# Row scales kept on chip, k's low parts doubled to 128 rows, and the q/k norm steps moved between engines

## The chip, the core and the metric

The kernel runs on one core of a Trainium2 chip. A core has TensorE (PE, matmuls; its weight loads are shown apart as PEld), VectorE (DVE), ScalarE (ACT), GpSimd (POOL) and SyncE (SP), which here only issues transfers. Engines run their own instructions in order and wait for each other by semaphores. The metric is device time in microseconds for one execution; lower is better. Beside it stands a profile of one execution, with the start and length of each instruction.

## What is computed

One block on a sequence of 1024 tokens with 1024 features, in float32: a norm, a mixer made of stick-breaking attention and a gated linear recurrence, a second norm, and an MLP with a squared ReLU. Cut to what matters here:

```python
h = rms_norm(x, norm1_g)
q, k, v, xl, gl = split(h @ w_in)              # 512 features each
q = rms_norm(q per head of 64, q_norm_g)
k = rms_norm(k per head of 64, k_norm_g)
# per head, causal:
z = (q @ k.T) / sqrt(64)
w = sigmoid(z) * suffix_product(sigmoid(-z))   # where key < query
attn = w @ v
lru = rg_lru(conv(xl)) * gelu(gl)
x = x + concat(attn, lru) @ w_out
x = x + square(relu(rms_norm(x) @ w_up)) @ w_down
```

There are eight heads of 64 features. `rms_norm` multiplies by one over the root of the mean square.

## The kernel before

**Precision.** Most products are made from a high and a low part of each operand: a value is rounded to the matmul's format (the high part, a copy on ScalarE) and the remainder is the low part (`lo_part`, L60, a subtraction on VectorE or GpSimd). `mm3` (L70 to L73) then adds three matmuls: low by high, high by low, high by high.

**Stages.** First x is loaded, transposed and scaled (`norm1_pair`), and the q, k, v of the first pair of heads are made. Then comes the recurrent unit (`lru_tile`), whose result goes to DRAM (`lru_d`). Then comes a stage in which attention, the projections of the other three pairs and the gates are woven together: `ORDER` (L34) lists these pieces by hand, with `A` for one head and 256 queries, `I` for a projection of 256 tokens, `G` for a gate, `W` and `O` for weight loads and `Y` for sums of MLP weights made by transfers. Last come the output projection and the MLP. The framework places the instructions of each engine in an order of its own, worked out from its estimate of their times, so instructions of several pieces alternate on an engine.

**A projection step** (`in_proj`, four per pair of heads, 16 in all) works on 256 tokens:

- TensorE makes q, k, v for two tiles of 128 tokens (`pd`, L201); ScalarE copies q and k to `raw` with the row's scale (L203), and v's parts are taken at L205 and L206.
- VectorE squares `raw` (L209), sums over 64 features (L211) and runs `rsqrt_mean` (L88): a scale and a guess made from the bits (L92, L93), then three Newton steps of three operations each on eight columns (L95, L96, L97). VectorE then scales `raw` (L213), and GpSimd multiplies q by the gains (L214).
- q's high and low parts go side by side into 128 columns (`qs`). k's high part is written twice (`ks`, L222), its low part once (`kl`, L223, on GpSimd).
- TensorE transposes them (L228, L233, L237), and `qT`, `kH` and `kL` are copied out (L229, L234, L238). In `kL` the two heads lie one above the other, 64 rows each.

**Attention** (L414) makes `z` for 128 queries and up to 512 keys from two matmuls: L431 with all 128 rows (q's high and low parts by k's high part twice) and L432 with the head's 64 rows (q's high part by k's low part). On the diagonal L434 adds the mask. ScalarE takes two sigmoids (L436, L437), VectorE a running product (L441), GpSimd multiplies (L442), TensorE transposes the weights (L452), and L461 multiplies them with v.

**A gate** (L479) loads the 512 row scales of its tokens, spread over 128 partitions, from `rs_d` in DRAM (L483) into a buffer of the tag `raw`, loads the recurrent result (L484), projects (L485), scales (L487), and goes on with the gelu. The same row scales were held on chip as `rsb` (L353) during the recurrent unit and given up after it.

Of the kernel before, what the change touches and what calls it, by code (L numbers as in the profile page):

```python
# [9 lines left out]
F32 = mybir.dt.float32  # L10
F32R = mybir.dt.float32r
# [8 lines left out]
P = 128  # L20
# [23 lines left out]
def kernel(ctx, tc, x, norm1_g, w_in, conv_w, conv_b, w_rg, b_rg, w_ig, b_ig,  # L44
# [39 lines left out]
    def bank(pl, shape, name):  # L84
        return pl.tile([P] + shape, F32, tag=pl.name, name=name)


    def rsqrt_mean(ssq, n, cols):  # L88
        v = small.tile([P, 8], F32, tag="rs_v", name="rs_v")[:, :cols]
        y = small.tile([P, 8], F32, tag="rs_y", name="rs_y")[:, :cols]  # L90
        m = small.tile([P, 8], F32, tag="rs_m", name="rs_m")[:, :cols]
        nc.vector.tensor_scalar(v, ssq, 1.0 / n, EPS, op0=ALU.mult, op1=ALU.add)  # L92
        nc.vector.tensor_scalar(y.bitcast(I32), v.bitcast(I32), -0.5, float(0x5F3759DF), op0=ALU.mult, op1=ALU.add)  # L93
        for _ in range(3):
            nc.vector.scalar_tensor_tensor(m, y, -0.5, v, op0=ALU.mult, op1=ALU.mult)  # L95
            nc.vector.tensor_tensor(m, m, y, op=ALU.mult)  # L96
            nc.vector.scalar_tensor_tensor(y, m, 1.5, y, op0=ALU.add, op1=ALU.mult)  # L97
        return y
# [52 lines left out]
    hTh = hp.tile([P, KC, S], F32R, name="hTh")  # L151
    hTl = hp.tile([P, KC, S], F32R, name="hTl")
    qkvE = pool(left1, "qkvE")
    wp = pool(left1, "wp", bufs=8)
    mp = pool(left1, "misc")

# [31 lines left out]

    def in_proj_open(p, qp):
        return (qp.tile([P, 2, S], F32R, tag="qT", name=f"qT{p}"), qp.tile([P, 2, S], F32R, tag="kH", name=f"kH{p}"),  # L190
                qp.tile([P, S], F32R, tag="kL", name=f"kL{p}"), qp.tile([P, NT, 2, P], F32R, tag="vv", name=f"vv{p}"))

    def in_proj(p, qkv, ws, tp):
        qT, kH, kL, vv = qkv
        raw = mp.tile([P, 2, 4, HD], F32, tag="raw", name=f"raw{p}{tp}", bufs=2)
        for tt in range(2):
            t = 2 * tp + tt
            pd = bank(ps_d, [384], f"pd{p}{t}")
            for kc in range(KC):
                wh, wl = ws[kc]  # L200
                mm3(pd, hTh[:, kc, t * P:(t + 1) * P], hTl[:, kc, t * P:(t + 1) * P], wh, wl, kc == 0, kc == KC - 1)  # L201
            rs = rstd1[:, t:t + 1]
            nc.scalar.mul(raw[:, tt].rearrange("p a d -> p (a d)"), pd[:, 0:256], rs)  # L203
            pvv = pd[:, 256:384].rearrange("p (h d) -> p h d", h=2)
            nc.scalar.mul(vv[:, t, :, 0:HD], pvv, rs)  # L205
            nc.vector.scalar_tensor_tensor(vv[:, t, :, HD:P], pvv, rs, vv[:, t, :, 0:HD].bitcast(F32), op0=ALU.mult, op1=ALU.subtract)  # L206
        sq = mp.tile([P, 8, HD], F32, tag="sq", name=f"sq{p}{tp}")
        raw8 = raw.rearrange("p t a d -> p (t a) d")
        nc.vector.tensor_tensor(sq, raw8, raw8, op=ALU.mult)  # L209
        ssq = small.tile([P, 8], F32, tag="ssq8", name=f"ssq{p}{tp}")  # L210
        nc.vector.tensor_reduce(ssq, sq, axis=AX.X, op=ALU.add)  # L211
        rstd = rsqrt_mean(ssq, HD, 8)
        nc.vector.tensor_tensor(raw8, raw8, rstd.unsqueeze(2).broadcast_to([P, 8, HD]), op=ALU.mult)  # L213
        nc.gpsimd.tensor_tensor(raw[:, :, 0:2, :], raw[:, :, 0:2, :], qkg, op=ALU.mult)  # L214
        qs = mp.tile([P, 2, 2, 2, HD], F32R, tag="qs", name=f"qs{p}{tp}")
        ks = mp.tile([P, 4, 2, HD], F32R, tag="ks", name=f"ks{p}{tp}")
        kl = mp.tile([P, 2, 2, HD], F32R, tag="kl", name=f"kl{p}{tp}")
        for h in range(2):
            nc.scalar.copy(qs[:, :, h, h, :], raw[:, :, h, :])
            lo_part(nc.vector, qs[:, :, h, 1 - h, :], raw[:, :, h, :], qs[:, :, h, h, :])  # L220
        for tt in range(2):
            nc.scalar.copy(ks[:, 2 * tt:2 * tt + 2], raw[:, tt, 2:4, :].unsqueeze(2).broadcast_to([P, 2, 2, HD]))  # L222
            lo_part(nc.gpsimd, kl[:, tt], raw[:, tt, 2:4, :], ks[:, 2 * tt:2 * tt + 2, 0, :])  # L223
        cols = slice(256 * tp, 256 * tp + 256)
        pq = bank(ps_t, [2, 256], f"pq{p}{tp}")
        for h in range(2):
            for tt in range(2):
                nc.tensor.matmul(pq[:, h, tt * P:(tt + 1) * P], qs[:, tt, h].rearrange("p a d -> p (a d)"), identr, start=True, stop=True)  # L228
        nc.scalar.copy(qT[:, :, cols], pq)  # L229
        pk = bank(ps_t, [2, 256], f"pk{p}{tp}")  # L230
        for h in range(2):
            for tt in range(2):
                nc.tensor.matmul(pk[:, h, tt * P:(tt + 1) * P], ks[:, 2 * tt + h].rearrange("p a d -> p (a d)"), identr, start=True, stop=True)  # L233
        nc.vector.tensor_copy(kH[:, :, cols], pk)  # L234
        pl = bank(ps_t, [256], f"pl{p}{tp}")
        for tt in range(2):
            nc.tensor.matmul(pl[:, tt * P:(tt + 1) * P], kl[:, tt].rearrange("p a d -> p (a d)"), identr, start=True, stop=True)  # L237
        nc.vector.tensor_copy(kL[:, cols], pl)  # L238


    right1 = ExitStack()
# [108 lines left out]

    lstack = ExitStack()
    lp = pool(lstack, "lru", bufs=2, side="right")
    rsb = lp.tile([P, S], F32, name="rsb", bufs=1)  # L353
    for ch in range(2):
        nc.sync.dma_start(rsb[:, 512 * ch:512 * ch + 512], rs_row[:, 512 * ch:512 * ch + 512].broadcast_to([P, 512]))
    bd = {}
# [57 lines left out]
    def attention(p, h, c, qkv):  # L414
# [4 lines left out]
        for r in (2 * c, 2 * c + 1):  # L419
            n = (r + 1) * P  # L420
            wps = {}
            nxt = None
            qr = slice(r * P, (r + 1) * P)
            for k0 in range((n - 1) // 512 * 512, -1, -512):
                kn = min(n - k0, 512)
                diag = k0 + kn == n
                g = ap.tile([P, 516], F32, tag="g", name=f"g{p}{h}{r}{k0}", bufs=NG)
                w = ap.tile([P, 512], F32, tag="w", name=f"w{p}{h}{r}{k0}", bufs=NW)
                wps[k0 // 512] = w
                z = bank(ps_z, [512], f"z{p}{h}{r}{k0}")[:, :kn]  # L430
                nc.tensor.matmul(z, qT[:, h, qr], kH[:, h, k0:k0 + kn], start=True, stop=False)  # L431
                nc.tensor.matmul(z, qT[hs, h, qr], kL[hs, k0:k0 + kn], start=False, stop=not diag)  # L432
                if diag:
                    nc.tensor.matmul(z[:, kn - P:kn], identb, maskb, start=False, stop=True)  # L434
                    nc.gpsimd.memset(g[:, kn:kn + 1], 1.0)
                nc.scalar.activation(g[:, :kn], z, AF.Sigmoid, scale=-1.0)  # L436
                nc.scalar.activation(w[:, :kn], z, AF.Sigmoid)  # L437
                if not diag:
                    nc.vector.tensor_copy(g[:, kn:kn + 1], nxt)
                gr = g[:, :kn][:, ::-1]  # L440
                nc.vector.tensor_tensor_scan(gr, gr, gr, g[:, kn:kn + 1], op0=ALU.mult, op1=ALU.bypass)  # L441
                mark(nc.gpsimd.tensor_tensor(w[:, :kn], w[:, :kn], g[:, 1:kn + 1], op=ALU.mult))  # L442
                nxt = g[:, 0:1]
            wrow.append(wps)
# [34 lines left out]
    def gate(c, ch):  # L479
        s0 = 512 * ch  # L480
        y = mp.tile([P, 512], F32, tag="raw", name=f"gx{c}{ch}", bufs=2)
        hs = mp.tile([P, 512], F32, tag=("ks", "kl")[c % 2], name=f"hl{c}{ch}")
        nc.sync.dma_start(y, rs_row[:, s0:s0 + 512].broadcast_to([P, 512]))  # L483
# [3 lines left out]
        nc.vector.tensor_tensor(y, pd, y, op=ALU.mult)  # L487
# [387 lines left out]
```

## Time and profile before

| | us |
|---|---|
| three runs | 1215.89, 1217.34, 1218.22 |
| median | 1217.34 |
| profiled execution | 1218.14 |
| its span | 1216.4 |

| engine | busy, share of the span | instructions |
|---|---|---|
| TensorE | 95% | 5410 |
| its weight loads | 78% | 5410 |
| VectorE | 74% | 1182 |
| ScalarE | 47% | 991 |
| GpSimd | 48% | 472 |

The shares are means over stages with different limits. TensorE's granted clock is 0.969 of full speed on the mean. Matmuls are pipelined and their ends are modelled, so the records of neighbours overlap; what one costs is read from its start to the next one's start. Where a row names what an engine waited for, that is the semaphore that came last in the profile; "issue" is idle time for which the profile shows no wait.

### The profile page before, as it was taken

To read this page: it belongs to the slowest core of one execution; us is meant where nothing else is said; L and a number is where in the kernel's file an instruction comes from. 1 tells how busy PE (TensorE), PEld (TensorE's weight loads), DVE (VectorE), ACT (ScalarE), POOL (GpSimd) and SP (SyncE) were. 2 spreads that over 40 slices of the span, in tenths; PEclk is the share of its full clock that TensorE was granted. 3 is DMA by queue.
4 is the path that set the end of the run, shared out by engine and by line. 5 is a ranking of instruction groups with operands and counts; after the bars stand their busy time and mean duration, and the time that the engine had idled before them with its cause. 6 is when DMAs were issued, how large, how long until landed. Compare 5 with 4: busy or idle time off the path is not lost.

```text
span 1216.4 us, 15273 instructions
## 1 busy us (share of the span) xinstructions
PE 1150.6 (95%) x5410; PEld 948.0 (78%) x5410; DVE 897.3 (74%) x1182; ACT 568.5 (47%) x991; POOL 586.5 (48%) x472
## 2 busy tenths in 40 slices
PE   7998899999999988998999989889999999999998
PEld 7976777789987766886888767678887887878887
DVE  6889997999898788226387769685843876699663
ACT  7554475665665564144433554233334335733331
POOL 1356764574355566102645746533317368483240
PEclk9999999799999978998999989989999999999999
DMA  8110026824505275200453788944412345442531
GB/s 262 48 49 35 18 96 130 227 66 145 122 5 112 89 256 181 101 1 35 141 188 130 201 241 287 224 142 139 141 35 87 122 144 191 158 148 73 193 132 69
DMA packets 91659, 157.05 MB, mean 129 GB/s; under 512 B 8848, under 2 KB 27328, under 8 KB 91584
## 3 DMA queue, kind: packets, MB, share of 16 engines
q1 hardware_dynamic: 79040, 122.54, 30.5%
q0 software_dynamic: 12544, 33.56, 11.8%
q8 instruction: 42, 0.69, 0.2%
q14 instruction: 33, 0.27, 0.1%
HBM read 145.58 MB, written 44.04 MB: 156 GB/s over the span
## 4 chain that ended last, share of the span: by engine, by line
PE 69%; DVE 13%; issue 8%; DMA 3%; POOL 3%; ACT 3%; SPq 0%; DVEq 0%; ACTq 0%; POOLq 0%
PE p L633 22%; PE pa L633 11%; PE pb L633 5%; PE pc L633 4%; PE pd L71 3%; PE pd L72 3%; PE pd L73 3%; PE po L71 3%; PE po L72 2%; PE po L73 2%; PE av L461 2%; PE z L432 2%; PE pw L452 2%; DVE g L441 2%; DVE sl_u L60 2%
## 5 line engine op out<-in xcount | busy, mean ns | idle before, releaser
L442 POOL TENSOR_TENSOR w<-w,g 128x128 f32<-128x128 f32 (+3 forms) x96 | 99.7, 1044 | 107.7 <-DVE g L441 52.7
L60 DVE TENSOR_TENSOR ml_p<-rp,mh_p 128x1024 fp32r<-128x1024 f32 x56 | 110.3, 1971 | 28.1 <-ACT mh_p L544 28.1
L441 DVE TENSOR_TENSOR_SCAN g<-g 128x128 f32<-128x128 f32 (+3 forms) x96 | 112.6, 1185 | 8.0 <-ACT g L436 5.4
L544 ACT CAST sh_p<-U 128x1024 fp32r<-128x1024 f32 x48 | 50.5, 1051 | 131.0 <-PE pa L633 59.2
L633 PE MATMUL pa<-mh_p,sl_p 128*128 128x512 f32 x256 | 100.7, 393 | 7.1 <-DVE sl_p L60 6.8
L767 POOL TENSOR_TENSOR rp<-rp,qp 128x1024 f32<-128x1024 f32 x24 | 69.0, 2876 | 70.3 <-DMA qp<-in_w_down_dram 39.8
L633 PE MATMUL pa<-ml_p,sh_p 128*128 128x512 f32 x256 | 100.3, 392 | 0.0
L633 PE MATMUL pa<-mh_p,sh_p 128*128 128x512 f32 x256 | 100.1, 391 | 0.0
L71 PE MATMUL pd<-wh_p,hTl 128*128 128x384 f32 x256 | 90.9, 356 | 7.3 <-DVE vv L206 5.0
L72 PE MATMUL pd<-wl_p,hTh 128*128 128x384 f32 x256 | 89.8, 351 | 0.1
L73 PE MATMUL pd<-wh_p,hTh 128*128 128x384 f32 x256 | 88.3, 345 | 0.0
L60 DVE TENSOR_TENSOR sl_p<-U,sh_p 128x1024 fp32r<-128x1024 f32 x38 | 63.4, 1668 | 30.7 <-ACT sh_p L544 30.7
L737 POOL TENSOR_TENSOR ru<-ru,rv 128x1024 f32<-128x1024 f32 x16 | 43.8, 2769 | 58.9 <-DMA rv<-sum_u 58.8
L544 ACT CAST mh_p<-rp 128x1024 fp32r<-128x1024 f32 x56 | 58.7, 1048 | 21.3 <-POOL rp L767 14.6
L633 PEld LDWEIGHTS pa<-mh_p,sl_p 128*128 128x128 f32 x256 | 48.5, 189 | 18.2 <-DVE sl_p L60 7.5
L662 POOL TENSOR_TENSOR U<-U 128x512 f32<-128x512 f32 x32 | 47.0, 1501 | 32.0 <-ACT U L660 32.0
L456 ACT CAST wth<-pw 128x512 fp32r<-128x512 f32 (+1 forms) x80 | 42.4, 545 | 38.0 <-PE pw L452 24.8
L436 ACT ACTIVATE g<-z 128x384 f32<-128x384 f32 (+3 forms) x96 | 47.8, 497 | 22.9 <-PE z L434 10.4
L71 PEld LDWEIGHTS pd<-wh_p,hTl 128*128 128x128 f32 x256 | 49.4, 193 | 11.0 <-DVE vv L206 6.7
L660 ACT ACTIVATE U<-U 128x512 f32<-128x512 f32 x48 | 30.0, 628 | 58.6 <-DVE U L721 31.1
L60 DVE TENSOR_TENSOR wtl<-pw,wth 128x512 fp32r<-128x512 f32 (+1 forms) x80 | 49.5, 629 | 9.5 <-ACT wth L456 8.9
L633 PEld LDWEIGHTS pa<-mh_p,sh_p 128*128 128x128 f32 x256 | 48.5, 189 | 10.2
(325 smaller groups left out, 3566.7 us busy)
## 6 DMA issues: line engine op xcount, KB each, us to landing
sum_u<-in_w_up_dram POOLq DMA_DIRECT2D x8, 2048.0 KB, 12.7
sum_d<-in_w_down_dram POOLq DMA_DIRECT2D x8, 2048.0 KB, 13.3
rp<-in_w_down_dram SPq DMA_DIRECT2D x32, 512.0 KB, 4.1
rp<-sum_d SPq DMA_DIRECT2D x24, 512.0 KB, 5.4
ra<-in_w_up_dram SPq DMA_DIRECT2D x16, 512.0 KB, 4.4
qp<-in_w_down_dram SPq DMA_DIRECT2D x16, 512.0 KB, 4.2
wr_p<-in_w_in_dram SPq DMA_DIRECT2D x24, 192.0 KB, 5.8
xt<-in_x_dram SPq DMA_DIRECT2D x8, 512.0 KB, 7.5
```

The lines of the kernel that those rows point to most:

```text
L60: ins = eng.tensor_tensor(lo, src, hi.bitcast(F32), op=ALU.subtract)
L71: nc.tensor.matmul(ps, al, bh, start=start, stop=False)
L72: nc.tensor.matmul(ps, ah, bl, start=False, stop=False)
L73: nc.tensor.matmul(ps, ah, bh, start=False, stop=stop)
L436: nc.scalar.activation(g[:, :kn], z, AF.Sigmoid, scale=-1.0)
L441: nc.vector.tensor_tensor_scan(gr, gr, gr, g[:, kn:kn + 1], op0=ALU.mult, op1=ALU.bypass)
L442: mark(nc.gpsimd.tensor_tensor(w[:, :kn], w[:, :kn], g[:, 1:kn + 1], op=ALU.mult))
L544: nc.scalar.copy(hl[0], src)
L633: nc.tensor.matmul(ps, x_, y_, start=start and n == 0, stop=stop and n == 2, skip_group_check=True)
L662: mark(nc.gpsimd.tensor_tensor(c, c, c, op=ALU.mult))
L737: mark(nc.gpsimd.tensor_tensor(r, r, q, **add))
L767: mark(nc.gpsimd.tensor_tensor(r, r, q, **add))
```

## The change

There are four edits.

1. The row scales `rsb` live in the pool of the transposed input to the end of attention. Gates read them there, and the transfer of L483 is gone.
2. k's low part is written twice (`kl` with the shape of `ks`), transposed per head, and kept as `kL` with 128 rows for each head. The second matmul of `z` uses all 128 rows; it now adds q's low part by k's low part too, a term that was left out before.
3. The Newton steps of the norms of q and k run on GpSimd: one scaling and three times four operations in place of nine on VectorE. The other norms keep them on VectorE.
4. The squares for these norms are taken on ScalarE.

```diff
-    def rsqrt_mean(ssq, n, cols):
+    def rsqrt_mean(ssq, n, cols, gp=False):
...
+        if gp:
+            nc.gpsimd.tensor_scalar(v, v, -0.5, 0.0, op0=ALU.mult, op1=ALU.add)
+            for _ in range(3):
+                nc.gpsimd.tensor_tensor(m, y, y, op=ALU.mult)
+                nc.gpsimd.tensor_tensor(m, m, v, op=ALU.mult)
+                nc.gpsimd.tensor_scalar(m, m, 1.0, 1.5, op0=ALU.mult, op1=ALU.add)
+                nc.gpsimd.tensor_tensor(y, y, m, op=ALU.mult)
+            return y
...
+    rsb = hp.tile([P, S], F32, name="rsb")
...
-                qp.tile([P, S], F32R, tag="kL", name=f"kL{p}"), ...
+                qp.tile([P, 2, S], F32R, tag="kL", name=f"kL{p}"), ...
...
-        nc.vector.tensor_tensor(sq, raw8, raw8, op=ALU.mult)
+        nc.scalar.activation(sq, raw8, AF.Square)
...
-        rstd = rsqrt_mean(ssq, HD, 8)
+        rstd = rsqrt_mean(ssq, HD, 8, True)
...
-            lo_part(nc.gpsimd, kl[:, tt], raw[:, tt, 2:4, :], ks[:, 2 * tt:2 * tt + 2, 0, :])
+            lo_part(nc.gpsimd, kl[:, 2 * tt:2 * tt + 2], raw[:, tt, 2:4, :].unsqueeze(2).broadcast_to([P, 2, 2, HD]),
+                    ks[:, 2 * tt:2 * tt + 2])
...
-        pl = bank(ps_t, [256], f"pl{p}{tp}")
-        for tt in range(2):
-            nc.tensor.matmul(pl[:, tt * P:(tt + 1) * P], kl[:, tt].rearrange("p a d -> p (a d)"), identr, start=True, stop=True)
-        nc.vector.tensor_copy(kL[:, cols], pl)
+        pl = bank(ps_t, [2, 256], f"pl{p}{tp}")
+        for h in range(2):
+            for tt in range(2):
+                nc.tensor.matmul(pl[:, h, tt * P:(tt + 1) * P], kl[:, 2 * tt + h].rearrange("p a d -> p (a d)"), identr, start=True, stop=True)
+        nc.vector.tensor_copy(kL[:, :, cols], pl)
...
-    rsb = lp.tile([P, S], F32, name="rsb", bufs=1)
...
-                nc.tensor.matmul(z, qT[hs, h, qr], kL[hs, k0:k0 + kn], start=False, stop=not diag)
+                nc.tensor.matmul(z, qT[:, h, qr], kL[:, h, k0:k0 + kn], start=False, stop=not diag)
...
-        nc.sync.dma_start(y, rs_row[:, s0:s0 + 512].broadcast_to([P, 512]))
...
-        nc.vector.tensor_tensor(y, pd, y, op=ALU.mult)
+        nc.vector.tensor_tensor(y, pd, rsb[:, s0:s0 + 512], op=ALU.mult)
```

More of the change, by code (lines that the diff above doesn't have):

```diff
@@ L190, in in_proj_open @@
         return (qp.tile([P, 2, S], F32R, tag="qT", name=f"qT{p}"), qp.tile([P, 2, S], F32R, tag="kH", name=f"kH{p}"),
-                qp.tile([P, S], F32R, tag="kL", name=f"kL{p}"), qp.tile([P, NT, 2, P], F32R, tag="vv", name=f"vv{p}"))
+                qp.tile([P, 2, S], F32R, tag="kL", name=f"kL{p}"), qp.tile([P, NT, 2, P], F32R, tag="vv", name=f"vv{p}"))
     def in_proj(p, qkv, ws, tp):
@@ L216, in in_proj @@
         ks = mp.tile([P, 4, 2, HD], F32R, tag="ks", name=f"ks{p}{tp}")
-        kl = mp.tile([P, 2, 2, HD], F32R, tag="kl", name=f"kl{p}{tp}")
+        kl = mp.tile([P, 4, 2, HD], F32R, tag="kl", name=f"kl{p}{tp}")
         for h in range(2):
```

## The prediction

> **What bounds the kernel now.** I read the page's busy table first, then the busy times by stretch. The change touches three stages only: the first projection (to about 62 us), the recurrent unit (to 137 us) and attention with the projections and gates woven into it (137 to 462 us). Output projection and MLP keep their code, so I look at attention.
>
> ```profile
> span 1216.4 us, 15273 instructions
> ```
> ```profile
> 137.00:200.00 63.00, 56.55 (x299) 45.83 (x297) 58.83 (x113) 32.92 (x83) 36.67 (x52) 0.97 0.37 100
> 200.00:260.00 60.00, 57.25 (x280) 44.83 (x280) 53.46 (x75) 38.42 (x89) 36.16 (x47) 0.83 0.62 161
> 260.00:420.00 160.00, 158.28 (x926) 135.81 (x924) 139.13 (x281) 93.30 (x232) 80.24 (x119) 0.99 0.34 85
> 420.00:462.00 42.00, 34.06 (x168) 25.68 (x166) 33.91 (x47) 25.39 (x55) 25.26 (x25) 0.84 0.61 215
> sum 325.00, PE 306.14 PEld 252.15 DVE 285.33 ACT 190.03 POOL 178.33; mean PE 76.53 PEld 63.04 DVE 71.33 ACT 47.51 POOL 44.58
> ```
>
> The columns are stretch and length, then busy time (instructions) of TensorE, weight loads, VectorE, ScalarE and GpSimd, the granted clock, the DMA share and GB/s. From 260 to 420 us TensorE is busy 158.28 of 160 us: that stretch ends when TensorE's instructions are through. In the other 165 us of attention it lacks 6.4, 2.8 and 7.9 us, 17.1 in all, and VectorE, with 58.83 of 63 us in the first, is the other engine that can be late. Over all 325 us VectorE is busy 285.33, or 88%, GpSimd 178.33, or 55%.
>
> A busy TensorE is not one that works. The timeline of its matmuls (start, duration, line, operation; durations overlap, so the cost is read from start to start) shows it around L432, the product of k's low parts, which uses 64 of 128 rows:
>
> ```profile
> 338.96 0.33 PE L72 MATMUL pd<-wl_p,hTh 128*128 128x384 f32 x1
> 339.13 0.40 PE L431 MATMUL z<-kH,qT 128*128 128x512 f32 x1
> 339.46 0.49 PE L432 MATMUL z<-kL,qT 64*128 64x512 f32 x1
> 339.88 0.45 PE L73 MATMUL pd<-wh_p,hTh 128*128 128x384 f32 x1
> 340.16 0.34 PE L71 MATMUL pd<-wh_p,hTl 128*128 128x384 f32 x1
> ```
> ```profile
> 342.00 0.36 PE L431 MATMUL z<-kH,qT 128*128 128x256 f32 x1
> 342.30 0.38 PE L432 MATMUL z<-kL,qT 64*128 64x256 f32 x1
> 342.61 0.23 PE L434 MATMUL z<-maskb,identb 128*128 128x128 bf16 x1
> 342.65 0.42 PE L71 MATMUL pd<-wh_p,hTl 128*128 128x384 f32 x1
> 342.90 0.33 PE L72 MATMUL pd<-wl_p,hTh 128*128 128x384 f32 x1
> ```
> ```profile
> 395.65 0.39 PE L71 MATMUL pgl<-hTh,wl_gl 128*128 128x512 f32 x1
> 395.88 0.39 PE L72 MATMUL pgl<-hTl,wh_gl 128*128 128x512 f32 x1
> ```
> ```profile
> 339.45 0.18 PEld L432 LDWEIGHTS z<-kL,qT 64*128 64x128 f32 x1 [0.31 <-issue]
> 339.98 0.19 PEld L71 LDWEIGHTS pd<-wh_p,hTl 128*128 128x128 f32 x1
> ```
>
> A 512-column matmul with 128 rows starts its successor 0.23 us later (395.65 to 395.88), a 384-column one after 0.17 (338.96 to 339.13). Around the 64-row product, L431 takes 0.33 until L432 starts, L432 takes 0.42, and the matmul behind it 0.28. That is 0.10 + 0.19 + 0.11 = 0.40 us too much. With 256 columns and the mask product L434 behind: 0.30 and 0.31 against half of 0.23, so 0.185 + 0.195; L434 and its successor take 0.04 + 0.25, against about 0.23 for a quarter of 0.23 and 0.17, so 0.06: 0.44 us. The weight-load rows show why: L432's load begins only after an idle 0.31 us put down to "issue", while L71's load at 339.98 runs under the matmul of 339.88. I take 0.41 us for each, near the lower.
>
> **The change, part by part.**
>
> *Full rows for k's low parts.*
>
> ```profile
> L432 PE MATMUL z<-kL,qT 64*128 64x384 f32 (+3 forms) x96 | 44.4, 463 | 0.0
> ```
> ```profile
> 260.00:420.00 160.00, 19.61 (x45) 8.22 (x45) 0.99 0.34 85
> ```
>
> There are 96 such products. With 128 rows L432 has the shape of L431, which follows a projection matmul after 0.17 us (338.96 to 339.13). So I expect 96 x 0.41 = 39.4 us of TensorE's time to go. 45 products lie in the stretch where TensorE sets the end: 45 x 0.41 = 18.5 us, counted in full. The other 51 (20.9 us) lie where TensorE also waits for others; I count half, 10.5, with ends 0 and 20.9.
>
> The Trainium skill, "TensorE: Matmul & The Clock Gate", section "What overlaps and what doesn't", says that a weight load runs under a matmul only when the two use different row groups. By it, a full-row load behind a full-row matmul would wait as well, and nothing would be won; the load of 339.98 under a full-row matmul says otherwise. I keep it as a rival below.
>
> The price is on three engines. TensorE transposes the low parts in four products a step instead of two; VectorE's copy to kL (L238) doubles; so does GpSimd's subtraction (L60 to kl).
>
> ```profile
> L209 DVE TENSOR_TENSOR sq<-raw 128x512 f32<-128x512 f32 x11 | 9.9, 903 | 3.5 <-ACT raw L203 3.5
> L96 DVE TENSOR_TENSOR rs_m<-rs_m,rs_y 128x8 f32<-128x8 f32 x36 | 9.9, 275 | 0.8
> L97 DVE SCALAR_TENSOR_TENSOR rs_y<-rs_m,rs_y 128x8 f32<-128x8 f32 x36 | 8.7, 243 | 0.7
> L95 DVE SCALAR_TENSOR_TENSOR rs_m<-rs_y,rs_v 128x8 f32<-128x8 f32 x36 | 7.7, 214 | 0.7
> L234 DVE CAST kH<-pk 128x512 fp32r<-128x512 f32 x12 | 8.1, 674 | 0.0
> L238 DVE CAST kL<-pl 128x256 fp32r<-128x256 f32 x12 | 4.8, 404 | 0.0
> ```
> ```profile
> L60 POOL TENSOR_TENSOR kl<-raw,ks 128x128 fp32r<-128x128 f32 x32 | 17.4, 565 | 7.8 <-PE pl L237 6.4 <-ACT wth L456 1.1 <-ACT w L437 0.3
> L214 POOL TENSOR_TENSOR raw<-raw,qkg 128x256 f32<-128x256 f32 x16 | 11.8, 739 | 41.6 <-DVE raw L213 13.4 <-DVE rs_m L96 13.4 <-DVE rs_m L95 13.1
> L435 POOL MEMSET g<- 128x1 f32 x64 | 7.1, 126 | 0.5
> L404 POOL COPY ext<-ext 128x3 f32<-128x3 f32 x4 | 1.2, 297 | 12.4 <-DVE ext L405 6.3 <-DVE u L391 3.5 <-PE pl L237 2.5
> ```
> ```profile
> 340.69 0.34 PE L237 MATMUL pl<-identr,kl 128*128 128x128 f32 x2
> 340.86 0.39 PE L71 MATMUL pd<-wh_p,hTl 128*128 128x384 f32 x1
> ```
>
> Two transposes of L237 take 0.17 us (340.69 to 340.86), so 16 steps x 2 more x 0.085 = +2.7 us, counted in full. L238 becomes the size of L234: 0.674 - 0.404 = +0.27 us a step. L60's kl becomes the size of L214: 0.739 - 0.565 = +0.17 us, twice a step.
>
> *Norms.* From VectorE go L209 (0.903) and nine Newton operations, three each of L95, L96 and L97: 3 x (0.275 + 0.243 + 0.214) = 2.20 us. Less the copy's 0.27 that is 2.83 us a step, 34 over the 12 steps in attention: VectorE falls from 285 to 251 us, and against a stage of 325 - 29 = 296 us that is 85%, below today's 88%. So VectorE doesn't become the bound, and TensorE's gain can be had. By itself the relief is worth only what TensorE waits for VectorE; out of those 17.1 us I take 2 (ends 0 and 7).
>
> The square goes to ScalarE:
>
> ```profile
> L664 ACT ACTIVATE U<-U 128x512 f32<-128x512 f32 x32 | 20.0, 630 | 0.8
> ```
>
> 0.63 us for the same 128x512, 12 x 0.63 = 7.6 us on an engine that has 190.03 of 325 us busy; that idle time hides it.
>
> GpSimd takes 13 small operations a step, a shape that it doesn't have now. Bounds are 0.126 us (memset of one column, L435) and 0.297 (copy of three, L404). Drawing the line from L214 (256 columns) through kl (128) down to 8 gives, with these means, 0.40, so the ends are 0.126 and 0.40; the memset and the copy are nearest in width, but one reads nothing and the other is a mean of four: I take 0.25. A step is 13 x 0.25 = 3.3 us (1.6 to 5.2), 12 steps in attention 39, and with kl's growth 43: GpSimd rises to 221 of 296 us, 75%. It has the room, but it adds a wait: L213 on VectorE now waits for GpSimd's last multiplication, and behind L213 stand the scans (L441) and v's low parts (L206), which TensorE needs. What the wait has to beat is today's chain:
>
> ```profile
> 179.26 0.16 DVE L92 TENSOR_SCALAR rs_v<-ssq 128x8 f32<-128x8 f32 x1
> 184.16 0.69 DVE L213 TENSOR_TENSOR raw<-raw,rs_y 128x512 f32<-128x512 f32 x1
> ```
>
> From L92 to L213 pass 4.9 us, because other VectorE work is put between. 3.3 us fit in, with one of w's products (L442) between them. I charge 0.2 us for each of 16 steps: +3.2 (ends 0 and 54, the slower rival).
>
> *Gates.* Eight loads of the row scales and their landing go.
>
> ```profile
> DVE gx L487 <- DMA gx<-rs_d: 4.5, 3, 3.3
> ```
> ```profile
> SPq L483 <- POOL kl L60: 18.6, 3, 9.8
> ```
>
> VectorE waits 4.5 us for them in three gates; I take 3 (ends 0 and 4.5), as the gate's own matmuls end little earlier. The queue of SyncE also stood 18.6 us in L483 until GpSimd had left the buffer `raw`, with stores and weight loads behind it. That wait moves to VectorE's L487, which writes the same buffer; the matmuls of L185 between cover it. If they didn't, those up to 18.6 us would stand on VectorE.
>
> `rsb` and the larger kL hold their memory until attention ends. I cost that at nothing: the first loads of the output projection, which take that space over, have TensorE's last attention work to hide them; without that cover they would come late by about a landing, for which L487's longest wait of 3.3 us is my estimate.
>
> *Sum:* -18.5 - 10.5 + 2.7 - 2 + 3.2 - 3 = -28.1 us. The profiled execution took 1218.14 us, 1.7 above its span and 0.8 above the median 1217.34. 1218.1 - 28.1 = **1190 us**.
>
> **The rivals.**
>
> *A, the forecast:* 1172 to 1203 us. For it: TensorE's 98.9% in 260 to 420 us, and L431 as a full-row product without delay.
>
> *B, VectorE pays back.* L209, with two inputs from SBUF, takes 0.903 us where L234, of the same size from PSUM, takes 0.674: a third more, with GpSimd busy 55% of the time. If each added GpSimd microsecond (43) lengthens VectorE's work by 0.34 / 0.55 = 0.6, 26 of the 34 us come back, VectorE stands at 277 of 296 us (94%), and the gain holds only in the dense stretch, less some 5 us: -13.5 + 2.7 + 3.2 - 3 = -10.6, or 1208 us. Against it: the new operations are eight columns wide. The Trainium skill, "GPSIMD Engine Reference", section "Engine selection", advises VectorE for elementwise work, with GpSimd about half as fast on two inputs, and its "Specifications" name shared SBUF interfaces; this rival is what that would do here.
>
> *C, the edit doesn't do what it says:* the delay belongs to a second product into one bank to reloading the same q, or to any load that waits for the matmul before it, not to 64 rows. Then 29 us fall away: 1219 us. The last is what the Trainium skill's rule of row groups, above, would do. Against it: projection matmuls add 24 times into one bank at 0.17 us.
>
> ```profile
> L442 POOL TENSOR_TENSOR w<-w,g 128x512 f32<-128x512 f32 x48 | 60.4, 1260 | 66.8 <-DVE g L441 38.9 <-ACT w L437 8.4 <-DVE rs_y L97 6.6
> ```
>
> *D, slower:* L213 waits in earnest. If four of w's products stand between GpSimd's small operations, a step is 3.3 + 4 x 1.26 us = 8.3 us, 3.4 later than today's 4.9; 16 x 3.4 = 54 us in place of 3.2: 1218.1 - 31.3 + 54 = 1241 us. It turns the sign from 31.3 / 16 = 2.0 us a step on.
>
> **How the numbers follow.** A 0.62, B 0.18, C 0.08, D 0.12. About 0.2%, 2.4 us, is what a measurement of this kernel can tell from no change. Faster: A, nearly all of B and little of C, 0.81; within: most of C, 0.06; slower: D and some of C, 0.13. The range takes in A, B and C: up to 1219 us; below, all 39.4 us, gates 4.5 and VectorE 7, less 2.7: 1218.1 - 48.2 = 1170, and 2 us for the bounds: 1168.
>
> **What would show it.** L432 with 128 rows, its start-to-start at 0.23 us for 512 columns, and no idle "issue" before its load: the first step. L95 to L97 only 24 times, L209 gone, VectorE near 251 us in attention: the relief. Attention some 28 us shorter and the stages behind it unchanged: the sum. A wait of L213 for GpSimd above 2 us a step, or VectorE above 94% busy, would prove me wrong; so would a moved order of instructions that takes TensorE's place in the dense stretch.

## The result and the profile after

The change makes the kernel slower, by 0.8%. In seven runs its median is 1226.06 us (1223.63 to 1228.35); the kernel before had 1218.08 us beside them. The ratio is 1.0078, with a 95% interval of 1.0057 to 1.0099. The profiled execution took 1228.15 us, span 1226.4. Predicted were 1190 us and a range that ended at 1219.

The page's head and busy table of the kernel after:

```profile
span 1226.4 us, 15347 instructions
...
PE 1133.1 (92%) x5442; PEld 952.9 (78%) x5442; DVE 865.7 (71%) x1022; ACT 572.7 (47%) x1007; POOL 644.8 (53%) x680
```

TensorE's share fell from 95% to 92%, VectorE's from 74% to 71%, and GpSimd's rose from 48% to 53%. TensorE has less to do, and VectorE's and GpSimd's busy times went the way that was forecast, but the end still came later.

Busy time by stretch of the kernel after, laid 12 us later than the stretches shown of before, because attention begins 12 us later (columns as there; two of the four stretches, and the sum over all four, 149 to 470 us):

```profile
149.00:212.00 63.00, 56.96 (x312) 49.71 (x312) 53.66 (x78) 38.14 (x93) 49.93 (x91) 0.92 0.36 94
272.00:432.00 160.00, 149.31 (x937) 135.22 (x935) 126.47 (x207) 102.62 (x255) 115.71 (x220) 0.97 0.32 79
sum 321.00, PE 280.88 PEld 250.06 DVE 259.84 ACT 194.35 POOL 225.96; mean PE 70.22 PEld 62.51 DVE 64.96 ACT 48.59 POOL 56.49
```

The sums are close to the forecast: VectorE 259.84 us (251 expected), GpSimd 225.96 (221 expected). TensorE is busy 280.88 us of this stage instead of 306.14. But the four stretches span 321 us, where 296 were expected for the stage. The timelines of both kernels give its exact ends, the first product of `z` and the last `ob` (the last subtraction of attention). First before, then after:

```profile
137.25 0.22 PE L431 MATMUL z<-kH,qT 128*128 128x128 f32 x1
...
461.48 0.42 DVE L467 TENSOR_TENSOR ob<-av,ot 64x256 f32<-64x256 f32 x1 [1.17 <-ACT ot L466]
```

```profile
149.16 0.22 PE L441 MATMUL z<-kH,qT 128*128 128x128 f32 x1
...
468.94 0.42 DVE L477 TENSOR_TENSOR ob<-av,ot 64x256 f32<-64x256 f32 x1 [1.19 <-ACT ot L476]
```

Attention went from 324.2 to 319.8 us: 4.4 shorter, not 28. And it begins 11.9 us later. The stages behind add 2.5 us in this one profile.

The largest thing that the eye finds ahead of attention is the third projection step. VectorE and GpSimd in the timeline, before and then after (the last column is the idle time and what ended it):

```profile
46.73 0.17 DVE L92 TENSOR_SCALAR rs_v<-ssq 128x8 f32<-128x8 f32 x1
...
49.94 0.69 DVE L213 TENSOR_TENSOR raw<-raw,rs_y 128x512 f32<-128x512 f32 x1
```

```profile
45.69 0.17 DVE L92 TENSOR_SCALAR rs_v<-ssq 128x8 f32<-128x8 f32 x1
...
46.16 0.20 POOL L95 TENSOR_SCALAR rs_v<-rs_v 128x8 f32<-128x8 f32 x1 [4.60 <-DVE rs_y L93]
...
52.46 0.20 POOL L100 TENSOR_TENSOR rs_y<-rs_y,rs_m 128x8 f32<-128x8 f32 x1
...
58.43 0.72 POOL L60 TENSOR_TENSOR wl_xl<-wr_xl,wh_xl 128x256 fp32r<-128x256 f32 x1 [4.77 <-ACT wh_xl L173]
59.12 0.20 POOL L97 TENSOR_TENSOR rs_m<-rs_y 128x8 f32<-128x8 f32 x1
...
64.48 0.69 DVE L222 TENSOR_TENSOR raw<-raw,rs_y 128x512 f32<-128x512 f32 x1
```

From L92 to the scaling of `raw` passed 3.21 us; now 18.79 pass. GpSimd does its instructions in order, and between two Newton operations (52.46 and 59.12) stands a subtraction of other weights that waited 4.77 us for ScalarE. It looks like the cause. The first experiment below shows that the late begin of attention is there without it. Over the whole of the kernel after, up to 470 us, the scaling waits far less for GpSimd than this step suggests (total, times, longest):

```profile
DVE raw L222 <- POOL rs_y L100: 12.8, 8, 2.9
```

The instructions themselves are no longer in the same order. Compared by operation and tile name, the longest common sequences keep at most 4997 of TensorE's 5442 instructions in the old order, 857 of ScalarE's 1007, and 862 of the 1022 that VectorE now has; buffers of one name count as the same here, so fewer are truly in place. The framework has planned all engines anew.

### The profile page after: what moved, and what is told of

Same layout as the page of the kernel before. It is cut to its first block, busy times and chain, and to the rows that moved or that the text cites. A ratio compares the mean times of both kernels' runs of the same rounds, so it can differ in the third digit from the quotient of the medians.

```text
span 1226.4 us, 15347 instructions
## 1 busy us (share of the span) xinstructions
PE 1133.1 (92%) x5442; PEld 952.9 (78%) x5442; DVE 865.7 (71%) x1022; ACT 572.7 (47%) x1007; POOL 644.8 (53%) x680
## 4 chain that ended last, share of the span: by engine, by line
PE 57%; DVE 17%; issue 8%; DMA 8%; POOL 6%; ACT 4%; SPq 0%; DVEq 0%; POOLq 0%; ACTq 0%
PE p L642 18%; PE pa L642 10%; PE pb L642 4%; PE pc L642 4%; PE po L71 2%; PE po L72 2%; PE po L73 2%; DVE g L451 2%; PE av L471 2%; DVE sl_p L60 2%; DVE ml_p L60 1%; DVE wtl L60 1%; PE pd L71 1%; PE pd L72 1%; PE pd L73 1%
## 5 line engine op out<-in xcount | busy, mean ns | idle before, releaser
L451 DVE TENSOR_TENSOR_SCAN g<-g 128x128 f32<-128x128 f32 (+3 forms) x96 | 115.7, 1220 | 15.1 <-ACT g L446 13.0
L642 PEld LDWEIGHTS pa<-mh_p,sl_p 128*128 128x128 f32 x256 | 48.7, 190 | 19.2 <-DVE sl_p L60 9.1
L462 PE MATMUL pw<-ident,w 128*128 128x128 f32 x288 | 50.0, 294 | 12.9 <-DVE wtl L60 8.4
L471 PE MATMUL av<-wtl,vv 128*128 128x256 f32 (+1 forms) x160 | 45.9, 311 | 15.0 <-DVE wtl L60 8.6
L466 ACT CAST wth<-pw 128x512 fp32r<-128x512 f32 (+1 forms) x80 | 42.3, 547 | 33.0 <-PE pw L462 18.5
L642 PEld LDWEIGHTS pa<-ml_p,sh_p 128*128 128x128 f32 x256 | 48.6, 190 | 10.2
```

What stands on the lines that cost most here:

```text
L462: nc.tensor.transpose(pw[:, i * P:(i + 1) * P], wrow[rr][j // 4][:, j % 4 * P:(j % 4 + 1) * P], ident)
L471: nc.tensor.matmul(av[:, q0:256], vv[:, 2 * m + jj, h, :], wt[:, 256 * jj:256 * jj + 256 - q0], start=m == 0 and jj == 0 and wt is wtl, st ...
L642: nc.tensor.matmul(ps, x_, y_, start=start and n == 0, stop=stop and n == 2, skip_group_check=True)
```

## The experiments

Two parts had to be told apart: what an edit does to the hardware, and what the new order does that the framework makes after any edit. The recorded expectations number their theories:

- Theory 1: the norms come late, behind other GpSimd work.
- Theory 2: TensorE's freed time goes into waits for other engines.
- Theory 3: the load of the row scales, now early in SyncE's queue, holds up the recurrent unit's weights.
- Theory 4: the edits do what was forecast, but the moved order costs more than they bring.
- Theory 5: the moved work itself comes late on ScalarE and GpSimd, whatever the order.

Times below are "(ratio - 1) x 1218 us", beside the kernel before on the same chip.

**1. Parts of the change, each in the order that the framework gives it.** `e1_no_gp` is the kernel after with the Newton steps left on VectorE:

```diff
-        rstd = rsqrt_mean(ssq, HD, 8, True)
+        rstd = rsqrt_mean(ssq, HD, 8)
```

> The changed kernel with the Newton steps back on VectorE; the full rows, the squares on ScalarE and the row scales on chip stay. Theory 1 (the norms come late behind other GpSimd work, which delays the first projection by 12 us and makes VectorE and TensorE wait in attention): 1190 to 1202 us. Theory 2 (TensorE's freed time goes into waits for the chain sigmoid, running product, weights, whoever does the norms): 1216 to 1226 us. Theory 3 (the load of the row scales, now early in SyncE's queue, delays the recurrent unit's weights): 1222 to 1228 us, since that load stays.

`e2_rows` is the kernel before with edit 2 alone (`kl`, `kL` and the product), `e3_gp` with edit 3 alone, `e4_rsb` with edit 1 alone, `e8_sq` with edit 4 alone, whose core is:

```diff
-        nc.vector.tensor_tensor(sq, raw8, raw8, op=ALU.mult)
+        nc.scalar.activation(sq, raw8, AF.Square)
```

> The kernel before with the full rows for k's low parts alone (kl, kL and the second product of z with 128 rows). Theory 1: the freed 26 to 39 us of TensorE's time are had where nothing else is added: 1188 to 1200 us. Theory 2: 1212 to 1220 us, TensorE's idle time for VectorE in attention grows by about what its work shrinks. Theory 3: as theory 1.

> The kernel before with the Newton steps of q and k on GpSimd alone. Theory 1: 1230 to 1250 us, the first attention product starts some 8 to 12 us later than at 137 us. Theory 2: within 4 us of 1218. Theory 3: within 4 us of 1218.

> The kernel before with the row scales kept on chip to the end of attention alone, and the eight loads in the gates gone. Theory 1 and 2: 1212 to 1217 us, the gates' waits go. Theory 3: 1222 to 1230 us, SyncE waits some 11 to 19 us for the row scales' way through DRAM ahead of weight loads, and the recurrent unit starts some 4 us later.

> The kernel before with the squares of q and k on ScalarE alone. VectorE is relieved of 14 us in all. Theory 4: anything from 1212 to 1235 us, as the order moves on every engine. Theory 2: 1212 to 1218 us.

| kernel | median us | ratio (95%) | us |
|---|---|---|---|
| after | 1226.06 | 1.0078 (1.0057 to 1.0099) | +9.5 |
| `e1_no_gp` | 1220.63 | 1.0033 (1.0014 to 1.0053) | +4.0 |
| `e2_rows` | 1230.07 | 1.0107 (1.0070 to 1.0143) | +13.0 |
| `e3_gp` | 1246.07 | 1.0228 (1.0187 to 1.0270) | +27.8 |
| `e4_rsb` | 1219.93 | 1.0040 (1.0017 to 1.0062) | +4.9 |
| `e8_sq` | 1245.90 | 1.0230 (1.0196 to 1.0264) | +28.0 |

Each edit alone makes the kernel slower, the squares by as much as the Newton steps, and the four together (73.7 by their sum) cost only 9.5. It is hard to see how moving 16 squares of 0.9 us to an engine that is idle half of the time could cost 28 us by itself. So these times are taken as those of an edit and its order together, which say little of the edit; experiment 4 tests that.

No theory fits all of these runs. The first had `e1_no_gp` at 1190 to 1202 us and `e2_rows` at 1188 to 1200. The second fits `e1_no_gp`, but had `e2_rows`, `e3_gp` and `e8_sq` no higher than 1220, 1222 and 1218. The third just misses `e1_no_gp` (from 1222) and `e4_rsb` (from 1222) and misses `e2_rows` and `e3_gp` by far. `e8_sq` lies even above the 1235 that the fourth allowed.

`e1_no_gp` also takes away the reading of the third step. Its timeline shows:

```profile
50.73 0.69 DVE L222 TENSOR_TENSOR raw<-raw,rs_y 128x512 f32<-128x512 f32 x1
...
149.00 0.22 PE L441 MATMUL z<-kH,qT 128*128 128x128 f32 x1
...
461.55 0.42 DVE L477 TENSOR_TENSOR ob<-av,ot 64x256 f32<-64x256 f32 x1 [1.17 <-ACT ot L476]
```

The scaling of `raw` is 13.75 us earlier than after, and the first product of `z` comes at 149.00, as late as after's 149.16.

Theory 3 has a trace of its own: SyncE's queue waits 19.2 us in all for the row scales' way through DRAM in the kernel after, 18.0 in `e1_no_gp` and 17.2 in `e4_rsb`, against 1.8 before. But `e2_rows` has no such wait, and its first product of `z` still comes at 146.80, 9.6 us later than before. So this wait can't be the whole of it.

**2. The product alone, in an unchanged order.** `e5_both_heads` changes one line of the kernel before. Both heads' low parts lie one above the other in `kL`, so all 128 rows can be taken as they are. The product then also adds q's low part by the other head's low part. That term is small, low by low, but doesn't belong there, so this is a test and not a kernel that computes quite the same. No transpose, copy or subtraction is added, and all engines keep the order of before, instruction by instruction.

```diff
-                nc.tensor.matmul(z, qT[hs, h, qr], kL[hs, k0:k0 + kn], start=False, stop=not diag)
+                nc.tensor.matmul(z, qT[:, h, qr], kL[:, k0:k0 + kn], start=False, stop=not diag)
```

> The kernel before with one line changed: the second product of z takes all 128 rows of q and of kL as it stands (both heads' low parts), so that it also adds q's low part by the other head's low part. No other work is added and every engine keeps its instructions in the order of before. Theory 4 (full rows do what was forecast, but the edits moved the framework's order of instructions, and that costs more than they bring): 1185 to 1205 us. Theory 2 (freed TensorE time goes into other waits even in the same order): 1212 to 1218 us. Delay that is not due to the 64 rows: 1218 us.

Measured: 1213.56 us, ratio 0.9963 (0.9946 to 0.9981), -4.5 us. The timeline of its TensorE and weight loads, at the place that the prediction quotes:

```profile
337.40 0.39 PE L431 MATMUL z<-kH,qT 128*128 128x512 f32 x1
337.63 0.40 PE L432 MATMUL z<-kL,qT 128*128 128x512 f32 x1
337.87 0.34 PE L73 MATMUL pd<-wh_p,hTh 128*128 128x384 f32 x1
338.05 0.34 PE L71 MATMUL pd<-wh_p,hTl 128*128 128x384 f32 x1
...
339.71 0.44 PE L237 MATMUL pl<-identr,kl 128*128 128x128 f32 x2 [0.97 <-DVE kH L234]
339.98 0.39 PE L71 MATMUL pd<-wh_p,hTl 128*128 128x384 f32 x1
...
340.04 0.19 PEld L72 LDWEIGHTS pd<-wl_p,hTh 128*128 128x128 f32 x1
```

From L431 to L432 pass 0.23 us, from there to the next 0.24, then 0.18, where before it was 0.33, 0.42 and 0.28. The delay of 0.38 us is gone, so it did belong to the 64 rows. L432's load no longer waits: the row of before from 137 to 470 us (total, times, longest) has no counterpart in `e5_both_heads`.

```profile
PEld z L432 <- issue: 17.1, 68, 0.4
```

The load of 340.04 runs under the full-row matmul of 339.98. The Trainium skill, "TensorE: Matmul & The Clock Gate", section "What overlaps and what doesn't", lets a load overlap only where row groups differ; this trace disagrees with it for loads and matmuls that both use all rows.

A little further stands the answer to where the gain went: L237 now waits 0.97 us for VectorE's `kH`. Busy time in the dense stretch:

```profile
260.00:420.00 160.00, 150.46 (x948) 137.51 (x946) 142.55 (x286) 94.61 (x237) 82.62 (x123) 0.99 0.35 88
```

TensorE's 158.28 us fell to 150.46. The 12 pieces of attention in the middle of that stretch, from the 12th `ob` to the 24th, took almost as long as before, though. First before, then `e5_both_heads`:

```profile
275.60 0.43 DVE L467 TENSOR_TENSOR ob<-av,ot 64x256 f32<-64x256 f32 x1
...
398.37 0.43 DVE L467 TENSOR_TENSOR ob<-av,ot 64x256 f32<-64x256 f32 x1 [0.87 <-ACT ot L466]
```

```profile
275.98 0.43 DVE L467 TENSOR_TENSOR ob<-av,ot 64x256 f32<-64x256 f32 x1
...
397.53 0.43 DVE L467 TENSOR_TENSOR ob<-av,ot 64x256 f32<-64x256 f32 x1
...
455.34 0.42 DVE L467 TENSOR_TENSOR ob<-av,ot 64x256 f32<-64x256 f32 x1 [1.17 <-ACT ot L466]
```

That is 122.8 us before and 121.6 now. 31 of the 45 products lie there before, 12.7 us at the forecast's price, and 1.2 came. From the 11th `ob` to the 26th, which takes in nearly all of the stretch, it is 149.9 and 145.9 us: 4.0 came of the 16.8 that 41 products promised. The last eight pieces, where only half was counted, took 63.1 us before (398.37 to 461.48) and take 57.8 now. These are two single profiles, and they lie 7.2 us apart where the runs together give 4.5.

What TensorE waited for from 137 to 470 us (total, times, longest), before and then in `e5_both_heads`:

```profile
PE av L461 <- DVE wtl L60: 5.1, 4, 3.6
PE pgl L71 <- DVE gx L487: 2.0, 1, 2.0
PE av L461 <- DVE ob L467: 1.6, 2, 1.4
PE pl L237 <- DVE kH L234: 1.1, 1, 1.1
```

```profile
PE av L461 <- DVE wtl L60: 8.6, 8, 2.4
PE av L461 <- DVE ob L467: 6.6, 3, 3.5
PE pgl L71 <- DVE gx L487: 4.0, 2, 3.7
PE pl L237 <- DVE kH L234: 3.5, 3, 1.4
```

These four waits, all for VectorE, rose from 9.8 to 22.7 us; with all the other rows of that list, TensorE's waits rose from 22.6 to 43.4 us, as much as its busy time fell there (310.11 to 289.09). TensorE got through its matmuls sooner and then waited for results of VectorE, which came hardly sooner than before. The second theory, 1212 to 1218 us, had this right.

**3. The same question in two other orders.** `e6_prod_only` is `e2_rows` with the second product back on 64 rows, and `e7_after_64` is the kernel after with the same line put back. Each keeps the order of its partner.

```diff
-                nc.tensor.matmul(z, qT[:, h, qr], kL[:, h, k0:k0 + kn], start=False, stop=not diag)
+                nc.tensor.matmul(z, qT[hs, h, qr], kL[hs, h, k0:k0 + kn], start=False, stop=not diag)
```

> The kernel with full rows alone, with the second product back on 64 rows of the doubled kL: its order on every engine is that kernel's (1230 us), and so is the work for kl and kL. Theory 4: 1250 to 1265 us, so the product itself saves some 25 us there too and the new order with the doubled kl and kL costs 35 to 45. Theory 2: 1230 to 1238 us.

> The changed kernel with the second product on 64 rows of the doubled kL, in the changed kernel's order. Theory 4: 1245 to 1260 us. Theory 2: 1226 to 1234 us.

`e6_prod_only`: 1231.87 us, 1.0108 (1.0076 to 1.0141), against 1.0107 for its partner: nothing that can be told. `e7_after_64`: 1235.37 us, 1.0141 (1.0105 to 1.0176), against 1.0078: full rows are worth 7.7 us in after's order. These times lie in and just above the second theory's ranges (1230 to 1238 and 1226 to 1234 us), well below the fourth's. So the product with 128 rows is worth from nothing to about 8 us, by the order in which it stands, and 29 nowhere.

**4. Each edit in the order of before.** Here the place of every instruction that a kernel shares with the one before is held. At the end of the program, edges are laid between neighbours in before's order on each engine and in each queue of transfers. They fix the order of issue and, being of the kind `NoSync`, ask for no wait on the chip. The instructions that an edit adds fall where the framework puts them. Compared by operation and tile, the traces of all these runs have the shared instructions of TensorE, VectorE, ScalarE and GpSimd in before's order.

```diff
+    traced = list(nc.cur_bb.bb.instructions)
+    for row in rows:
+        for i, j in zip(row, row[1:]):
+            tc.add_manual_dep(traced[j], traced[i].name,
+                              mybir.DependencyInfo(mybir.DependencyClass.NoSync, mybir.DependencyReason.DATA), reason="order")
```

The list `rows` holds, for each engine and queue, the instructions in before's order. `p1_after` has all four edits, `p2_rows` edit 2, `p3_gp` edit 3, `p4_sq` edit 4, `p5_rsb` edit 1, and `p7_no_gp` all but edit 3.

> The changed kernel with all four edits, but each instruction that it shares with the kernel before keeps that kernel's place in its engine's order (edges that fix the order only, with no waits); just the new ones (squares, GpSimd's Newton steps, two more transposes a step) find a place between. Theory 4 (the moved order costs what the edits bring): 1195 to 1214 us, below before's 1217. Theory 5 (the moved work itself comes late on ScalarE and GpSimd, whatever the order of the rest): 1222 to 1240 us.

> Full rows with the doubled kl and kL alone, in the order of before (1230 us in its own order). Theory 4: 1212 to 1218 us, the 4 us of the one-line form less 2 to 3 us for transposes and copies. Theory 5 says nothing of it. If the doubled kl and kL cost 12 us by themselves: 1228 to 1232 us.

> The Newton steps on GpSimd alone, in the order of before (1246 us in its own order). Theory 4: 1214 to 1222 us. Theory 5: 1232 to 1250 us, VectorE waits at the scaling of raw (L213) for GpSimd's last step by 1 to 2 us in each of 16 steps.

> The squares on ScalarE alone, in the order of before (1246 us in its own order). Theory 4: 1210 to 1217 us, VectorE has 14 us less to do. Theory 5: 1230 to 1248 us, VectorE waits at the sum of squares (L211) for ScalarE.

> The row scales on chip alone, in the order of before (1220 us in its own order). If the loss was the order's: 1211 to 1217 us, the gates' waits for the transfer go. If the early place of the load in SyncE's queue isn't the order's doing: 1219 to 1224 us.

> The changed kernel's other three edits, with the Newton steps left on VectorE, in the order of before. If these steps on GpSimd are what makes the changed kernel slow where the order is kept (1230 us): 1206 to 1216 us. If the edits disturb each other otherwise: 1220 us or more.

| edit | ratio in before's order (95%) | us | in its own order, us |
|---|---|---|---|
| full rows and doubled low parts (`p2_rows`) | 1.0021 (0.9994 to 1.0049) | +2.6 | +13.0 |
| Newton steps on GpSimd (`p3_gp`) | 1.0143 (1.0113 to 1.0174) | +17.4 | +27.8 |
| squares on ScalarE (`p4_sq`) | 0.9969 (0.9952 to 0.9987) | -3.8 | +28.0 |
| row scales on chip (`p5_rsb`) | 0.9958 (0.9944 to 0.9972) | -5.1 | +4.9 |
| sum of the four | | +11.1 | +73.7 |
| all four (`p1_after`) | 1.0097 (1.0061 to 1.0134) | +11.8 | +9.5 |
| all but Newton (`p7_no_gp`) | 0.9951 (0.9932 to 0.9971) | -6.0 | +4.0 |

In a fixed order the account closes. The four add up to +11.1 us, and 11.8 are measured together; without the Newton steps the sum is -6.3, and -6.0 are measured. An order that the framework makes anew costs 10 to 32 us more in five of the six rows. For all four edits together it comes out level, since the two intervals (1.0061 to 1.0134 and 1.0057 to 1.0099) overlap. So the fifth theory has the Newton steps right (1235.16 us for `p3_gp`, 1230.15 for `p1_after`), and the fourth has the squares (1214.10 for `p4_sq`). `p7_no_gp` came as expected with 1210.30; `p2_rows` (1219.15) and `p5_rsb` (1210.64) missed their ranges by about a microsecond or less.

The same edits stand in `e1_no_gp` in the framework's order and in `p7_no_gp` in before's. The ends of attention in `p7_no_gp` show where that order loses its time:

```profile
137.54 0.22 PE L652 MATMUL z<-kH,qT 128*128 128x128 f32 x1
...
450.96 0.42 DVE L688 TENSOR_TENSOR ob<-av,ot 64x256 f32<-64x256 f32 x1 [1.17 <-ACT ot L687]
```

Attention takes 313.4 us here and 312.6 in `e1_no_gp`; its first product comes at 137.54 and at 149.00. So for these three edits the new order costs nothing inside attention and some 11 us ahead of it. With the Newton steps on GpSimd too, attention begins 8 us later in the kernel after than in `p1_after` (149.16 against 140.98) and is 8 us shorter (319.8 against 327.7), which is how the two come out level.

**5. The chain of small operations.** `p8_gp1` is `p3_gp` with one Newton step in place of three, 5 operations on GpSimd in place of 13.

```diff
-            for _ in range(3):
+            for _ in range(1):
                 nc.gpsimd.tensor_tensor(m, y, y, op=ALU.mult)
```

> The Newton steps on GpSimd alone in the order of before, cut from three to one (5 operations on GpSimd a step in place of 13; the norms are less exact). If the length of GpSimd's chain, 13 times 0.28 us from start to start, is what VectorE waits for: 1214 to 1224 us against 1235 with three, and VectorE's wait for the chain falls from 42 us to under 15. If it is the crossing between the engines, or GpSimd's other work between: 1230 to 1236 us.

Measured: 1211.05 us, 0.9955 (0.9938 to 0.9972), or -5.5 us where `p3_gp` has +17.4. It is faster than expected, and faster than the kernel before, but it leaves out two Newton steps, so its norms are less exact. Eight small operations a step are worth 22.9 us, 1.4 us in each of 16 steps. The profiled execution of `p8_gp1` took 1220.16 us, the longest of its nine, so its waits are if anything too long. They fell as expected, to under 15 us. The lists of waits up to 470 us (total, times, longest) name it, first of `p3_gp`, then of `p8_gp1` (L428 and L429 are the scaling, L213 before):

```profile
DVE raw L429 <- POOL rs_y L308: 41.8, 14, 4.8
```

```profile
DVE raw L428 <- POOL rs_y L307: 6.8, 4, 2.6
```

The first step of `p3_gp` in the timeline, where nothing stands between GpSimd's operations, shows the length:

```profile
27.37 0.17 DVE L300 TENSOR_SCALAR rs_v<-ssq 128x8 f32<-128x8 f32 x1
27.57 0.17 DVE L301 TENSOR_SCALAR rs_y<-rs_v 128x8 int32<-128x8 int32 x1
...
27.84 0.19 POOL L303 TENSOR_SCALAR rs_v<-rs_v 128x8 f32<-128x8 f32 x1 [8.48 <-DVE rs_y L301]
28.00 0.19 POOL L305 TENSOR_TENSOR rs_m<-rs_y 128x8 f32<-128x8 f32 x1
28.28 0.20 POOL L306 TENSOR_TENSOR rs_m<-rs_m,rs_v 128x8 f32<-128x8 f32 x1
...
31.15 0.20 POOL L308 TENSOR_TENSOR rs_y<-rs_y,rs_m 128x8 f32<-128x8 f32 x1
31.54 0.68 DVE L429 TENSOR_TENSOR raw<-raw,rs_y 128x512 f32<-128x512 f32 x1
```

An operation on eight columns lasts 0.20 us on GpSimd, and the next one, which needs its result, starts 0.28 after it. From VectorE's first small operation to the scaling pass 27.37 to 31.54, 4.17 us: 0.47 until GpSimd begins (0.20 to VectorE's second operation, 0.27 from there), 3.31 from its first to its last start, 0.39 until VectorE begins. Before, with the operations on VectorE, the third step took 3.21, the shortest of its 16; in `p3_gp` 4.17 is the shortest of 16. The mean over all 16 steps, taken in the same way from the timeline, is 5.7 us before and 7.2 in `p3_gp`.

**6. A version that beats both.** `p6_best` keeps what gained in a fixed order: the one line of `e5_both_heads`, the squares on ScalarE and the row scales on chip, in before's order. The Newton steps stay on VectorE, and k's low parts aren't doubled. As in `e5_both_heads`, the one line brings in the other head's low part.

```diff
-        nc.vector.tensor_tensor(sq, raw8, raw8, op=ALU.mult)
+        nc.scalar.activation(sq, raw8, AF.Square)
...
-                nc.tensor.matmul(z, qT[hs, h, qr], kL[hs, k0:k0 + kn], start=False, stop=not diag)
+                nc.tensor.matmul(z, qT[:, h, qr], kL[:, k0:k0 + kn], start=False, stop=not diag)
...
-        nc.vector.tensor_tensor(y, pd, y, op=ALU.mult)
+        nc.vector.tensor_tensor(y, pd, rsb[:, s0:s0 + 512], op=ALU.mult)
```

> In the order of before: the squares on ScalarE, the row scales on chip, and the full-row second product in its one-line form (both heads' low parts as they stand); no Newton steps on GpSimd, no doubled kl and kL. If the single gains add (3.6 for the product, 3.1 for the squares, 0 to 5 for the row scales): 1204 to 1211 us. If VectorE's chain swallows them: 1211 to 1215 us.

Measured: **1203.76 us**, ratio 0.9894 (0.9875 to 0.9912), -12.9 us; its parts, -4.5, -3.8 and -5.1, make -13.4. It was expected at 1204 to 1211 us if the single gains add.

## Why the prediction was wrong

Its terms beside what each edit did alone in before's order, in us:

| term | forecast | measured |
|---|---|---|
| full rows, dense stretch and elsewhere | -18.5 - 10.5 | -4.5 (`e5_both_heads`) |
| doubled low parts | +2.7 | +7.1 (`p2_rows` less `e5_both_heads`) |
| relief of VectorE | -2 | -3.8 (squares alone) |
| the wait of L213, with the relief of the Newton steps | +3.2 | +17.4 (`p3_gp`) |
| gates | -3 | -5.1 (`p5_rsb`) |
| sum | -28.1 | +11.1 |

**The first step that failed: "45 products lie in the stretch where TensorE sets the end: 45 x 0.41 = 18.5 us, counted in full."** The mechanism was right: the delay of about 0.4 us around a 64-row product, its cause, and that it goes with 128 rows (0.38 us gone at the place quoted). That a stretch in which TensorE is busy 158.28 of 160 us ends when TensorE is through was wrong. The prediction itself had shown that a busy TensorE isn't one that works, and then used the busy share as proof of a bound, for TensorE here and for VectorE's "85%, below today's 88%" later. The delays counted as busy were also slack: as they went, waits for VectorE took their place, 9.8 to 22.7 us in four rows, and 4.0 us of 16.8 came in nearly the whole of that stretch, 1.2 of 12.7 in its middle. In all, 4.5 us of the 39.4 that were to go reached the end, 11%, far below the lower of the bounds that had been put at 18.5 and 39.4.

**The second: "3.3 us fit in", hence 0.2 us a step.** The price of one operation was near: 0.28 from start to start against 0.25. What failed was the comparison with the 4.9 us from L92 to L213. That gap of the old kernel held the nine Newton operations themselves, 2.20 us by the prediction's own sum. Take them out and 2.7 us are left to cover a chain that takes 4.2 with both hand-offs. By that arithmetic the scaling comes 4.2 - 2.7 = 1.5 us a step later against the work around it; the means of 7.2 and 5.7 differ by as much, and the runs gave 17.4 / 16 = 1.1 at the end. The Trainium skill's advice in "GPSIMD Engine Reference", section "Engine selection", to leave elementwise work to VectorE, agrees with this outcome, but for a reason that the prediction didn't weigh: the length of a chain of dependent operations, not the speed of one.

**The third isn't among the terms: the order.** "A moved order of instructions that takes TensorE's place in the dense stretch" was named as a thing that would prove the forecast wrong, and was given neither a price nor a chance. The framework's new orders cost 10 to 32 us for the single edits; the largest is as much as the whole gain that was forecast. For the change as it stands, two ways of taking it apart are measured. In before's order the Newton steps alone turn -6.0 into +11.8. In the framework's orders the other three edits already stand at +4.0, 10 us above their value in a fixed order, and the Newton steps add 5.5 (1.0078 against 1.0033; the intervals just part). Both say that the change without Newton steps on GpSimd is better, and that in the framework's order it loses its gain. Why a given order is slower is not shown: the runs show only where it is. For the other three edits it lies ahead of attention (first product at 149.00 in `e1_no_gp`, 137.54 in `p7_no_gp`). Of the signs that the prediction named, a moved order was the one that came, though its loss doesn't lie in the dense stretch for these three edits: the scaling's wait for GpSimd in the kernel after, 12.8 us or 0.8 a step, and VectorE at 259.84 of 321 us, 81%, stayed below the 2 us and the 94% named.

**The small terms.** The doubled low parts cost 7.1 us, with an uncertainty of about 4 from the two intervals, where 2.7 were charged for the transposes alone. The larger copy to `kL` and the larger subtraction were charged only as busy time of engines with room, and whether it is one of them was not tried. The gates were worth 5.1 us (3.4 to 6.8 by the interval), near their upper end of 4.5. The squares brought 3.8 of a band from 0 to 7. These two had the right sign and about the right size; which of their waits gave the gain was not tried.

**The rivals.** The ends that the prediction gives A, 1172 and 1203 us, aren't worked out there. C (the delay isn't due to the 64 rows) is refuted by the 0.23 and 0.24 us of `e5_both_heads`, though its time, 1219, is near what `p2_rows` gave. B (VectorE pays back) needs longer operations on VectorE, 26 us in all. Matched by operation, tiles and shape up to 470 us, those that both kernels have lasted 1.0 us longer than before in `p3_gp`, and 10.0 us in the kernel after, 4.4 of them on the scaling of `raw`. So it plays no part in the Newton steps' 17.4 us, and at most a small one in the change. D had the mechanism: L213 waits in earnest, 41.8 us in `p3_gp`. It asked for operations of other work between GpSimd's, and set the sign to turn at 2.0 us a step. That point stood on gains of 31.3 us. With the gains as measured, 6.3 net of the doubled parts, it is 6.3 / 16 = 0.4 us a step, and 1.1 is far beyond.

## What to carry to other kernels

A busy share near 100% doesn't show the bound when the busy time holds delays that can be removed: ask when the results of the next engine arrive, and be ready for a gain far below what is taken away (here 11%). When a chain of operations moves to another engine, take its own length out of the gap that is meant to cover it, and add both hand-offs. Where a framework plans the order, test an edit with the old order held, since a new order alone can be worth more than the edit.

## What was not expected of the hardware

Dependent operations on eight columns follow each other on GpSimd at 0.28 us, though one lasts 0.20, and the hand-over from VectorE to GpSimd and back took 0.27 and 0.39 us from start to start (27.57 to 27.84 and 31.15 to 31.54 above). On VectorE the same chain ran at 0.20 us from start to start in the rows below (third step of before, Newton operations on eight columns):

```profile
47.14 0.17 DVE L95 SCALAR_TENSOR_TENSOR rs_m<-rs_y,rs_v 128x8 f32<-128x8 f32 x1
47.35 0.17 DVE L96 TENSOR_TENSOR rs_m<-rs_m,rs_y 128x8 f32<-128x8 f32 x1
47.55 0.17 DVE L97 SCALAR_TENSOR_TENSOR rs_y<-rs_m,rs_y 128x8 f32<-128x8 f32 x1
47.75 0.17 DVE L95 SCALAR_TENSOR_TENSOR rs_m<-rs_y,rs_v 128x8 f32<-128x8 f32 x1
```
